# Seven products of blocks for eight in the second layer's first MLP product, with its sums on VectorE and its squares on ScalarE

## The chip, the cores and the metric

The kernel runs on one core of one Trainium2 chip. The metric is device time in microseconds, the median of the runs of the kernel; lower is better. The engines are called by the names of the profile: PE (TensorE, matmuls), DVE (VectorE), ACT (ScalarE), POOL (GpSimd) and SP (SyncE, which here issues DMAs).

## The reference

One inference step of a backbone of two layers, in float32. There are 640 tokens: 512 latent ones and 128 of context, each group with its own modulation. The model width is 1024, the hidden width of the MLP 4096.

```python
def squared_relu_mlp(h, w1, w2):
    return jnp.square(jax.nn.relu(h @ w1)) @ w2

def modulate(x, g, shift, scale):
    return rmsnorm(x, g) * (1 + scale) + shift

def trunk_layer(x, mod, p, mix_fn):
    shift1, scale1, gate1, shift2, scale2, gate2 = jnp.split(mod, N_MOD, axis=-1)
    y, ctx_state = mix_fn(modulate(x, p['norm1'], shift1, scale1))
    x = x + gate1 * y
    x = x + gate2 * squared_relu_mlp(modulate(x, p['norm2'], shift2, scale2), p['w1'], p['w2'])
    return x, ctx_state
```

`mix_fn` holds four groups of heads (a convolution, a spatial gate, latent attention and windowed attention) between one input and one output projection. After the second layer comes a last norm. The change concerns `h @ w1` of the second layer, the squares behind it, and the norm and modulation that make its `h`.

## The kernel before

Features lie on partitions and tokens on columns: `x` and the modulated `h` are eight tiles of 128 features by 640 tokens. The tokens are worked on in two parts, `HALVES = ((0, 384), (384, 256))`.

Every operand of a matmul is kept as two tensors, a high part (the value rounded to the matmul's format) and a low part (what the rounding left). `mm3` (L239 to L243) issues three matmuls for a product: high by high (L241), high by low (L242), low by high (L243). One product of 128 by 128 weights thus costs three matmuls. `load_unit` (L228 to L234) brings 128 x 1024 weights by a DMA from SP into a `raw` tile (three buffers), casts them on ACT (L232) and subtracts on DVE (L233), or on POOL where `pool` is set, into an `hl` tile (four buffers) that holds both parts.

The MLP of a layer works in eight portions of 512 hidden features. `mlp1(j)` (L1072) makes four hidden tiles of 128 in both token parts: 24 matmuls a tile and part into a PSUM bank `w1`, then `mlp1_tile` (L1059) takes relu on ACT (L1067), squares once on POOL (L1068, full precision) and once on ACT (L1069, the high part), and subtracts on DVE (L1070, the low part). `mlp2(j)` (L1099) multiplies the four tiles with the second weights into the eight feature tiles of the output, again by parts, and `gate_add` (L383 to L386) adds each result times the gate to `x` on DVE. The loop at L1119 issues `mlp1(j + 1)` ahead of `mlp2(j)`, so that PE has a portion of the first product to do while the other engines make the low parts of the one before. `Modulate.step` (L334) makes `h` for one feature tile and one token part: two or one products on DVE (L350), the high part on ACT, the low part on DVE (L358). The second token part's steps stand behind the first tile of `mlp1(0)`.

Results in PSUM come from the pools `mm`, `fl` and `s2` with two buffers each; one of `s2` holds two banks. The program is written in the order of the stages, and a scheduler of the tile framework sets the order in each engine's queue by the dependences and by a model of durations. On the chip each engine then runs its own queue in that order and waits by semaphores.

## Time and profile before

| what | value |
| --- | --- |
| median of three runs | 1562.17 us |
| the three runs | 1557.77, 1564.02, 1562.17 us |
| span of the profiled execution | 1557.7 us |
| PE busy | 1491.2 us, 96% of the span |
| PE weight loads (beside PE) | 1434.7 us |
| DVE busy | 1034.4 us, 66% |
| ACT busy | 612.0 us, 39% |
| POOL busy | 293.3 us, 19% |

The span and the busy times come from one profiled execution, whose own time lies with the lowest of the three runs. Matmuls overlap in the pipeline, so the duration of one PE row is longer than the time that it adds; starts tell the pace. A row's bracket names how long the engine was idle just before it and which work released it. The second layer's MLP lies at about 1088 to 1548 us of the span.

### The profile page before, as it was taken

What the parts mean: (1) busy time and instruction counts of PE and PEld (TensorE: products, weight loads), DVE (VectorE), ACT (ScalarE), POOL (GpSimd) and SP (SyncE); (2) the same over time, 40 slices, a digit from 0 to 9 for tenths busy, and PEclk for the clock granted to TensorE, in tenths of its full rate; (3) what the DMA queues carried; (4) which work ended last, traced back from release to release, by engine and by line L of the source; (5) the groups of instructions that cost most, each with busy time, mean ns of one, the idle gap of its engine ahead of it and who ended that gap; (6) DMA issues with size and microseconds to landing.
All of it is one profiled execution on the core that took longest, in us unless ns stands there. A gap on an engine that the chain in (4) does not pass through costs nothing. (4 is left out here: it accounts for less than half of the span.)

```text
span 1557.7 us, 25473 instructions
## 1 busy us (share of the span) xinstructions
PE 1491.2 (96%) x9884; PEld 1434.7 (92%) x9884; DVE 1034.4 (66%) x2051; ACT 612.0 (39%) x1324; POOL 293.3 (19%) x309
## 2 busy tenths in 40 slices
PE   6898999989999999999999999998999999999997
PEld 2698989979999999999999988997999999999997
DVE  5988878869988777876467676776643433443444
ACT  3544556744222231222246455774532223223221
POOL 2133103343210110110021120224211011001002
PEclk9899999999999999999999999999999999999998
DMA  8544321323555444444212311021222222222211
GB/s 309 197 136 138 99 71 45 90 87 111 184 161 162 145 151 151 149 148 137 75 48 70 116 42 35 28 72 63 87 69 82 68 82 69 81 76 74 78 45 68
DMA packets 49816, 159.52 MB, mean 102 GB/s; under 512 B 6176, under 2 KB 10272, under 8 KB 49696
## 3 DMA queue, kind: packets, MB, share of 16 engines
q1 hardware_dynamic: 48032, 153.96, 30.7%
q10 hardware_dynamic: 1664, 3.93, 0.7%
q8 instruction: 78, 1.28, 0.3%
q14 instruction: 42, 0.34, 0.1%
HBM read 154.82 MB, written 3.05 MB: 101 GB/s over the span
## 5 line engine op out<-in xcount | busy, mean ns | idle before, releaser
L232 ACT CAST hl<-raw 128x1024 fp32r<-128x1024 f32 (+3 forms) x204 | 200.1, 983 | 400.4 <-PE w L243 320.1
L242 PE MATMUL w<-h,hl 128*128 128x256 f32 (+1 forms) x1024 | 317.3, 311 | 6.6 <-DVE h L358 6.6
L241 PE MATMUL w<-u,hl 128*128 128x384 f32 (+1 forms) x1024 | 317.4, 310 | 3.6 <-DVE x L386 3.5
L243 PE MATMUL w<-h,hl 128*128 128x256 f32 (+1 forms) x1024 | 317.9, 310 | 0.0
L243 PE MATMUL w<-u,hl 128*128 128x384 f32 (+1 forms) x1024 | 317.0, 310 | 0.0
L242 PE MATMUL w<-u,hl 128*128 128x384 f32 (+1 forms) x1024 | 316.9, 309 | 0.0
L241 PE MATMUL w<-h,hl 128*128 128x256 f32 (+1 forms) x1024 | 316.7, 310 | 0.0
L233 DVE TENSOR_TENSOR hl<-raw,hl 128x1024 fp32r<-128x1024 f32 (+3 forms) x184 | 216.0, 1176 | 106.4 <-ACT hl L232 106.1
L1068 POOL TENSOR_TENSOR rq<-rr 128x384 f32<-128x384 f32 (+1 forms) x128 | 110.0, 860 | 676.3 <-ACT rr L1067 629.3
L386 DVE SCALAR_TENSOR_TENSOR x<-w,mod,x 128x128 f32<-128x128 f32 (+1 forms) x384 | 154.8, 434 | 109.7 <-PE w L243 109.0
L242 PEld LDWEIGHTS w<-h,hl 128*128 128x128 f32 x1024 | 195.0, 190 | 8.3 <-DVE h L358 8.2
L241 PEld LDWEIGHTS w<-u,hl 128*128 128x128 f32 x1024 | 194.2, 190 | 4.5 <-DVE x L386 4.1
L243 PEld LDWEIGHTS w<-h,hl 128*128 128x128 f32 x1024 | 195.0, 190 | 0.0
L241 PEld LDWEIGHTS w<-h,hl 128*128 128x128 f32 x1024 | 194.9, 190 | 0.0
L242 PEld LDWEIGHTS w<-u,hl 128*128 128x128 f32 x1024 | 194.4, 190 | 0.0
L243 PEld LDWEIGHTS w<-u,hl 128*128 128x128 f32 x1024 | 194.2, 190 | 0.0
L167 DVE CUSTOM_DVE_ANT_0 junk<-adaw,cb,vec 128x1024 f32<-128x1024 f32 x84 | 115.3, 1373 | 65.5 <-DMA adaw<-in_wada 65.5
L1067 ACT ACTIVATE rr<-w 128x384 f32<-128x384 f32 (+1 forms) x128 | 55.9, 436 | 250.2 <-PE w L243 250.2
L1070 DVE TENSOR_TENSOR u<-rq,u 128x384 fp32r<-128x384 f32 (+1 forms) x128 | 67.8, 530 | 92.7 <-POOL rq L1068 92.6
L167 DVE CUSTOM_DVE_ANT_0 adaw<-adaw,cb,vec 128x1024 f32<-128x1024 f32 x84 | 115.1, 1370 | 1.3
L241 PE MATMUL fm<-h,hl 128*128 128x256 f32 (+1 forms) x288 | 92.2, 320 | 2.1 <-DVE u L533 2.1
L242 PE MATMUL fm<-h,hl 128*128 128x256 f32 (+1 forms) x288 | 90.0, 313 | 0.0
(264 smaller groups left out, 2571.2 us busy)
## 6 DMA issues: line engine op xcount, KB each, us to landing
raw<-in_wf SPq DMA_DIRECT2D x146, 512.0 KB, 3.5
adaw<-in_wada SPq DMA_DIRECT2D x84, 512.0 KB, 3.8
raw<-in_wo SPq DMA_DIRECT2D x24, 384.0 KB, 3.1
adan<-in_wnat SPq DMA_DIRECT2D x12, 512.0 KB, 8.4
raw<-in_wt SPq DMA_DIRECT2D x16, 384.0 KB, 3.2
x<-in_xT ACTq DMA_DIRECT2D x4, 640.0 KB, 7.5
raw<-in_wt SPq DMA_DIRECT2D x8, 288.0 KB, 2.9
raw<-in_wo SPq DMA_DIRECT2D x4, 512.0 KB, 3.7
```

What stands on the lines that cost most here:

```text
L167: nc.vector.tensor_tensor_reduce(out=raw if g else junk, in0=raw, in1=cb[:, g, :], op0=ALU.mult, op1=ALU.add, scale=1.0, scalar=vecs[l][:, ...
L232: nc.scalar.copy(hl[:, 0, :n], raw[:, :n])
L233: (nc.gpsimd if pool else nc.vector).tensor_sub(hl[:, 1, :n], raw[:, :n], f(hl[:, 0, :n]))
L241: nc.tensor.matmul(out, lhsT=lhs[0], rhs=rhs[0], start=start, stop=False)
L242: nc.tensor.matmul(out, lhsT=lhs[0], rhs=rhs[1], start=False, stop=False)
L243: nc.tensor.matmul(out, lhsT=lhs[1], rhs=rhs[0], start=False, stop=stop)
L386: nc.vector.scalar_tensor_tensor(out=x[:, m, t0:t0 + n], in0=ps[:, t0 - b0:t0 - b0 + n], scalar=mods[l][g][:, gate + m:gate + m + 1], in1= ...
L1067: nc.scalar.activation(r, ps[:, :n], AF.Relu)
L1068: nc.gpsimd.tensor_mul(q, r, r)
L1070: nc.vector.tensor_sub(ui[:, 1, t0:t0 + n], q, f(hh))
```

## The change

In the second layer, hidden tiles are taken in pairs, `Pair(p)` with p from 0 to 15. Pairs 0 and 1 stay plain. Pairs 2 to 15 use the scheme of Strassen in Winograd's form: the 1024 features are split in two halves of four tiles, the 640 tokens in two halves of 320 (`HT`), and the pair's two tiles are the two halves of the third dimension. Of a pair's eight products of blocks seven are left; each is 4 x 3 = 12 matmuls of 320 columns. The names of their moving operands are `b11`, `b21`, `b22` (halves of `h` itself), `t1`, `t2`, `t3` and `t4` (sums of halves).

- `Blocks` (a subclass of `Modulate`): `keep()` reserves space for `h` in full precision, one tile of it in the constant `cb`, and `step` then issues one more pass on ACT for each high part of `h`. `sums(s)`, for s from 0 to 3, makes the four sums on DVE and splits each into high part (ACT) and low part (DVE); the sum `t4` overwrites a quarter of `h`.
- `Pair.load` brings a pair's two units of weights; `w1` and `w2` make four weight tiles from them, with four sums of 128 x 512 on DVE: `wa` (raw), `ws23`, `ws14` (sums) and `w22` (128 x 512). They use the four `hl` buffers.
- `first`, `second` and `rest` issue the seven products into PSUM banks `qa`, `qb` and the double bank `qcd`, two of them on top of another. DVE adds and subtracts the products to the four blocks of the result, ACT takes relu; `square` makes both squares on ACT over 640 columns and the low part on DVE.
- `full(p)` issues a whole pair. The loop: two plain pairs, the sums, `mlp2(0)`, pairs 2 and 3, and then pair 2j + 2, `mlp2(j)`, pair 2j + 3.
- Plain pairs of the second layer square on ACT twice instead of on POOL and ACT. The first layer keeps POOL.
- In both layers the second modulation and the plain tiles go through the feature tiles in the order `K_PAIRS`. The constants `msk` and `rq` are loaded once in each layer, and pools are opened and closed by phase so that the MLP has space of its own (`me`).

The diff, cut to its core:

```diff
+K_PAIRS = (0, 4, 1, 5, 2, 6, 3, 7)
...
+                if self.hf is not None:
+                    nc.scalar.activation(self.hf[k % 4][:, k // 4, t0:t0 + n], t[:, o:o + n], AF.Identity,
+                                         bias=shift)
...
+    class Blocks(Modulate):
...
+        def sums(self, s):
+            if s == 0:
+                self.op = {k: [None] * 4 for k in ("b11", "b21", "b22", "t1", "t2", "t3", "t4")}
+            op = self.op
+            if s % 2 == 0:
+                t3 = phase["me"].tile([128, 2, 2, HT], F32R, tag="t3", bufs=1, name=nm("t3")) if s else \
+                    tb([128, 2, 2, HT], "t3")
+                for k, two in (("t2", ta([128, 2, 2, HT], "t2")), ("t3", t3), ("t1", ta([128, 2, 2, HT], "t1"))):
+                    op[k][s], op[k][s + 1] = two[:, 0], two[:, 1]
+            h1, h2 = self.h[s], self.h[4 + s]
+            op["b11"][s], op["b21"][s], op["b22"][s] = h1[:, :, :HT], h2[:, :, :HT], h2[:, :, HT:]
+            op["t4"][s] = h1[:, :, HT:]
+            fx = self.hf[s]
+            b11, b12, b21, b22 = fx[:, 0, :HT], fx[:, 0, HT:], fx[:, 1, :HT], fx[:, 1, HT:]
+            t3, t2_ = tmp2([128, HT], "t3"), tmp2([128, HT], "t2")
+            nc.vector.tensor_sub(t3, b12, b22)
+            nc.vector.tensor_sub(b12, b11, b12)
+            nc.vector.tensor_add(t2_, b22, b12)
+            nc.vector.tensor_sub(b21, b21, t2_)
+            for k, src in (("t2", t2_), ("t3", t3), ("t1", b12), ("t4", b21)):
...
-            nc.gpsimd.tensor_mul(q, r, r)
...
+            def plain(self, us, i, half, tail=None):
...
+                hh = ui[:, 0, t0:t0 + n]
+                nc.scalar.activation(r, ps[:, :n], AF.Relu)
+                nc.scalar.activation(hh, r, AF.Square)
+                if blocks:
+                    nc.scalar.activation(q, r, AF.Square)
+                else:
+                    nc.gpsimd.tensor_mul(q, r, r)
+                nc.vector.tensor_sub(ui[:, 1, t0:t0 + n], q, f(hh))
+            def load(self):
+                self.raw = []
+                for i in range(2):
+                    raw = rawp.tile([128, 2, 512], F32, tag="raw", name=nm("raw"))
+                    nc.sync.dma_start(out=raw, in_=wf[l, U_W1 + 2 * self.p + i].rearrange("p (a b) -> p a b", a=2))
+                    self.raw.append(raw)
+            def hl(self, src, n=2):
+                t = hlp.tile([128, 2, 2, 512], F32R, tag="hl", name=nm("hl"))
+                split(t[:, 0, :n], t[:, 1, :n], src)
+                return t
+            def w1(self):
+                self.wa = self.hl(self.raw[0])
+            def w2(self):
+                r1, r2 = self.raw
+                s23 = me.tile([128, 2, 512], F32, tag="s", bufs=2, name=nm("s"))
+                s14 = me.tile([128, 2, 512], F32, tag="s", bufs=2, name=nm("s"))
+                nc.vector.tensor_add(s14[:, 0], r2[:, 0], r2[:, 1])
+                nc.vector.tensor_add(s23[:, 0], r1[:, 0], s14[:, 0])
+                nc.vector.tensor_add(s23[:, 1], r1[:, 0], r2[:, 0])
+                nc.vector.tensor_add(s14[:, 1], r1[:, 1], s23[:, 0])
+                self.ws23 = self.hl(s23)
+                self.ws14 = self.hl(s14)
+                self.w22 = self.hl(r2[:, 1:2], 1)
+            def mul(self, ps, w, i, op, start):
+                for s in range(4):
+                    c = slice(128 * s, 128 * s + 128)
+                    b = mod.op[op][s]
+                    mm3(ps, (w[:, 0, i, c], w[:, 1, i, c]), (b[:, 0, :], b[:, 1, :]), start and s == 0, s == 3,
+                        not start)
+            def first(self):
+                self.a = bank("qa")[:, :HT]
+                self.mul(self.a, self.wa, 0, "b11", True)
+                self.q1 = me.tile([128, HT], F32, tag="q1", bufs=1, name=nm("q1"))
+                nc.scalar.copy(self.q1, self.a)
+            def second(self):
+                self.mul(self.a, self.wa, 1, "b21", False)
+                self.r[0] = tp([128, TOK], "rr")
+                nc.scalar.activation(self.r[0][:, :HT], self.a, AF.Relu)
+            def square(self, i):
+                r, u = self.r[i], self.u[i]
+                nc.scalar.activation(u[:, 0, :], r, AF.Square)
+                nc.scalar.activation(r, r, AF.Square)
+                nc.vector.tensor_sub(u[:, 1, :], r, f(u[:, 0, :]))
+            def rest(self):
+                bv = bank("qb")[:, :HT]
+                cd = bank2("qcd")
+                c, d = cd[:, 0, :HT], cd[:, 1, :HT]
+                self.mul(bv, self.ws23, 0, "t2", True)
+                v, w = tmp2([128, HT], "V"), tmp2([128, HT], "W")
+                nc.vector.tensor_sub(v, bv, self.q1)
+                self.mul(c, self.ws23, 1, "t3", True)
+                nc.vector.tensor_add(w, c, v)
+                self.second()
+                self.mul(d, self.ws14, 0, "t1", True)
+                r0, r1 = self.r[0], tp([128, TOK], "rr")
+                self.r[1] = r1
+                nc.vector.tensor_sub(r1[:, HT:], w, d)
+                self.mul(c, self.w22, 0, "t4", False)
+                nc.vector.tensor_add(r1[:, :HT], c, v)
+                nc.scalar.activation(r1, r1, AF.Relu)
+                self.square(1)
+                self.mul(d, self.ws14, 1, "b22", False)
+                nc.vector.tensor_sub(r0[:, HT:], d, v)
+                nc.scalar.activation(r0[:, HT:], r0[:, HT:], AF.Relu)
+                self.square(0)
+        def full(p):
+            x_ = Pair(p)
+            x_.load()
+            x_.w1()
+            x_.w2()
+            x_.first()
+            x_.rest()
+            return x_.u
...
-        prev = mlp1(0)
-        for j in range(8):
-            cur = prev
-            if j < 7:
-                prev = mlp1(j + 1)
-            mlp2(j, cur)
+        head = [Pair(p, None if blocks else [ta([128, 2, TOK], "u") for _ in range(2)]) for p in range(2)]
+        ws = [load_unit(wf[l, U_W1 + i], pool=True) for i in range(4)]
+        for half in range(2):
+            for i in range(4):
+                head[i // 2].plain(ws[2 * (i // 2):2 * (i // 2) + 2], i % 2, half)
+                if half == 0 and i == 0:
+                    for k in K_PAIRS:
+                        mod.step(1, k)
+        us = head[0].u + head[1].u
+        if blocks:
+            for s in range(4):
+                mod.sums(s)
+            mlp2(0, us)
+            us = full(2) + full(3)
+            for j in range(1, 8):
+                if j < 7:
+                    nxt_us = full(2 * j + 2)
+                mlp2(j, us)
+                if j < 7:
+                    us = nxt_us + full(2 * j + 3)
+            close_phase()
+            del phase["me"]
+        else:
+            for j in range(8):
+                cur = us
+                if j < 7:
+                    us = two_plain(j + 1)
+                mlp2(j, cur)
```

In the order of PE the first place is the joint between two pairs, pair 7 to pair 8. Before, at the joint between `mlp1(j + 1)` and `mlp2(j)`, the rows are these (`w1`, `w2`: PSUM tiles of the two products; `h`, `u`: their moving operands; `hl`: weights):

```order
L242 MATMUL w1_2040_14124<-h_1719_11446,hl_2036_14090 128x256
L243 MATMUL w1_2040_14124<-h_1719_11446,hl_2036_14090 128x256
L241 MATMUL w2_2045_14160<-u_1947_13359,hl_2044_14157 128x384 [waits Activation_49]
L242 MATMUL w2_2045_14160<-u_1947_13359,hl_2044_14157 128x384
L243 MATMUL w2_2045_14160<-u_1947_13359,hl_2044_14157 128x384 [waits DVE_49]
```

Now `qcd_1964` is the double bank of pair 7 and `qa_1979` the first bank of pair 8, whose weights are `hl_1973`; `hl_1960` is pair 7's tile `w22`:

```order
L249 MATMUL qcd_1964_13346<-t1_1784_11866,hl_1959_13324 128x320
L250 MATMUL qcd_1964_13346<-t1_1784_11866,hl_1959_13324 128x320
L248 MATMUL qa_1979_13461<-h_1703_11348,hl_1973_13443 128x320 [waits Activation_49]
L249 MATMUL qa_1979_13461<-h_1703_11348,hl_1973_13443 128x320
L250 MATMUL qa_1979_13461<-h_1703_11348,hl_1973_13443 128x320 [waits DVE_49]
...
L248 MATMUL qa_1979_13461<-h_1725_11464,hl_1973_13443 128x320
L248 MATMUL qcd_1964_13346<-h_1703_11348,hl_1960_13327 128x320 [waits DVE_49]
L249 MATMUL qcd_1964_13346<-h_1703_11348,hl_1960_13327 128x320
```

Before, the next product's weights are another buffer of four that come one at a time; now the ten matmuls that need the next pair's first weights stand between the sixth and the seventh product, t1 and t4, of the pair before, behind a wait for the cast (ACT) and one for the low part (DVE).

In the order of ACT the second place is the joint between pair 8 and the second product of portion 3. Before, at such a joint the casts of weights (L232) stand like this among the passes of `mlp1` (L1067, L1069):

```order
L232 CAST hl_2012_13889<-raw_2011_13887 128x1024 [waits DMAHW6_49,PE_49]
L232 CAST hl_2020_13956<-raw_2019_13954 128x1024 [waits DMAHW7_49,PE_49]
L232 CAST hl_2028_14023<-raw_2027_14021 128x1024 [waits DMAHW0_49,DVE_49,PE_49]
L232 CAST hl_2036_14090<-raw_2035_14088 128x1024 [waits DMAHW1_49,DVE_49,PE_49]
L1067 ACTIVATE rr_2014_13917<-w1_2013_13892 128x384 [waits PE_49,Pool_49]
L1069 ACTIVATE u_2007_13883<-rr_2014_13917 128x384 [waits Activation_49]
```

Now, from the cast of pair 8's `ws14` (`hl_1977`) to that of the second product's first weights (`hl_1988`); `rr_1967` and `rr_1968` are what relu is taken of in pair 7, `u_1951` and `u_1952` its results:

```order
L253 CAST hl_1977_13455<-s_1975_13447 128x1024 [waits DVE_49,PE_49]
L1215 ACTIVATE rr_1968_13401<-rr_1968_13401 128x640 [waits DVE_49]
L1186 COPY q1_1980_13474<-qa_1979_13461 128x320 [waits PE_49,Activation_49]
L1195 ACTIVATE u_1952_13307<-rr_1968_13401 128x640 [waits Activation_49]
L253 CAST hl_1978_13458<-raw_1972_13441 128x512 [waits DMAHW1_49,PE_49]
L1196 ACTIVATE rr_1968_13401<-rr_1968_13401 128x640 [waits Activation_49]
L1219 ACTIVATE rr_1967_13387<-rr_1967_13387 128x320 [waits DVE_49]
L1195 ACTIVATE u_1951_13306<-rr_1967_13387 128x640 [waits Activation_49]
L1196 ACTIVATE rr_1967_13387<-rr_1967_13387 128x640 [waits Activation_49]
L239 CAST hl_1988_13570<-raw_1987_13568 128x1024 [waits DMAHW2_49,PE_49]
```

Where four casts followed one another, the cast of the second product's first weights now stands behind the seven passes and the short cast that follow `hl_1977`, which itself waits for PE.

In the order of DVE the third place is the start of the MLP of the second layer, ahead of the low part of the second product's first weights. Before (`u`: results of `mlp1(0)`; `h_1719`: the last tile of `h`):

```order
L1070 TENSOR_TENSOR u_1722_11452<-rq_1748_11596,u_1722_11452 128x384 [waits Pool_49]
L358 SCALAR_TENSOR_TENSOR h_1719_11446<-mt_1745_11563,mod1_123,h_1719_11446 128x128 [waits Activation_49] x2
L1070 TENSOR_TENSOR u_1723_11453<-rq_1751_11627,u_1723_11453 128x384 [waits Pool_49]
L1070 TENSOR_TENSOR u_1724_11454<-rq_1754_11658,u_1724_11454 128x384 [waits Activation_49,Pool_49]
L233 TENSOR_TENSOR hl_1772_11793<-raw_1771_11791,hl_1772_11793 128x1024 [waits DMAHW6_49,PE_49,Activation_49]
L1070 TENSOR_TENSOR u_1721_11451<-rq_1757_11689,u_1721_11451 128x256 [waits Activation_49,Pool_49]
```

Now (`hl_1790` are the second product's first weights; L254 is the low part in `split`, L415 to L418 are the sums of `Blocks.sums`, L1145 the low part of a plain tile):

```order
L254 TENSOR_TENSOR t3_1782_11864<-t3_1785_11867,t3_1782_11864 128x320 [waits Activation_49]
L415 TENSOR_TENSOR t3_1787_11881<-hf_1702_11347 128x320 [waits DVE_49]
L1145 TENSOR_TENSOR u_1731_11483<-rq_1771_11797,u_1731_11483 128x256 [waits Activation_49]
L254 TENSOR_TENSOR h_1703_11348<-cb_89,h_1703_11348 128x320 [waits Activation_49]
L254 TENSOR_TENSOR h_1713_11405<-hf_1700_11345,h_1713_11405 128x320 [waits Activation_49]
L254 TENSOR_TENSOR t1_1784_11866<-hf_1701_11346,t1_1784_11866 128x320 [waits Activation_49]
L254 TENSOR_TENSOR h_1721_11452<-hf_1701_11346,h_1721_11452 128x320 [waits Activation_49]
L416 TENSOR_TENSOR hf_1702_11347<-hf_1702_11347 128x320 [waits DVE_49]
L254 TENSOR_TENSOR t3_1782_11864<-t3_1787_11881,t3_1782_11864 128x320 [waits Activation_49]
L417 TENSOR_TENSOR t2_1788_11882<-hf_1702_11347 128x320 [waits DVE_49]
L240 TENSOR_TENSOR hl_1790_11897<-raw_1789_11895,hl_1790_11897 128x1024 [waits DMAHW0_49,Activation_49]
```

Ahead of the first low part of weights for PE's next stage there are now the sums of `h` and their low parts, of which the last are shown.

## Rows read from the trace of the kernel before

**Rows 1.** Page, span and part 1: busy us, share of the span, instructions.

```profile
span 1557.7 us, 25473 instructions
...
PE 1491.2 (96%) x9884; PEld 1434.7 (92%) x9884; DVE 1034.4 (66%) x2051; ACT 612.0 (39%) x1324; POOL 293.3 (19%) x309
```

**Rows 2.** A stretch of the second MLP: busy us (instructions) by engine, clock, DMA.

```profile
1250.00:1300.00 50.00, 50.00 (x343) 50.00 (x342) 20.72 (x37) 12.88 (x21) 4.82 (x7) 1.00 0.23 74
```

**Rows 3.** PE in order of time, one tile pair: start us, duration us.

```profile
1298.73 0.34 PE L241 MATMUL w<-h,hl 128*128 128x384 f32 x1
...
1302.89 0.28 PE L241 MATMUL w<-h,hl 128*128 128x256 f32 x1
...
1305.76 0.34 PE L241 MATMUL w<-h,hl 128*128 128x384 f32 x1
```

**Rows 4.** PE in order of time, three matmuls of 320 columns and the next.

```profile
990.60 0.31 PE L241 MATMUL S<-kk,qq 128*128 128x320 f32 x1
...
991.04 0.28 PE L242 MATMUL out<-y,hl 128*128 128x256 f32 x1
```

**Rows 5.** DVE groups by shape, whole run: busy us, mean ns, idle before.

```profile
L233 DVE TENSOR_TENSOR hl<-raw,hl 128x1024 fp32r<-128x1024 f32 x144 | 179.5, 1248 | 96.7 <-ACT hl L232 96.6
...
L386 DVE SCALAR_TENSOR_TENSOR x<-w,mod,x 128x384 f32<-128x384 f32 x128 | 78.5, 613 | 64.6 <-PE w L243 64.6
L386 DVE SCALAR_TENSOR_TENSOR x<-w,mod,x 128x128 f32<-128x128 f32 x256 | 77.6, 345 | 45.1 <-PE w L243 44.4
...
L626 DVE TENSOR_TENSOR ct<-ct,fm 128x384 f32<-128x384 f32 x4 | 2.2, 554 | 1.7 <-PE fm L243 1.7
L247 DVE TENSOR_TENSOR y<-cy,y 128x640 fp32r<-128x640 f32 x4 | 3.3, 818 | 0.0
...
L233 DVE TENSOR_TENSOR hl<-raw,hl 128x512 fp32r<-128x512 f32 x4 | 2.8, 688 | 4.9 <-ACT hl L232 4.9
```

**Rows 6.** ACT groups by shape, whole run, same columns.

```profile
L232 ACT CAST hl<-raw 128x1024 fp32r<-128x1024 f32 x152 | 159.1, 1048 | 367.3 <-PE w L243 317.2 <-DMA raw<-in_wf 29.5 <-PE fm L243 8.7
L1069 ACT ACTIVATE u<-rr 128x384 fp32r<-128x384 f32 x64 | 33.6, 525 | 1.9
...
L1069 ACT ACTIVATE u<-rr 128x256 fp32r<-128x256 f32 x64 | 26.8, 419 | 0.1
...
L628 ACT ACTIVATE cy<-ct,vec 128x640 f32<-128x640 f32 x4 | 3.3, 823 | 0.0
...
L246 ACT CAST y<-cy 128x640 fp32r<-128x640 f32 x4 | 2.9, 723 | 3.1 <-DVE cy L639 3.1
...
L232 ACT CAST hl<-raw 128x512 fp32r<-128x512 f32 x4 | 2.6, 639 | 0.8 <-PE tm L243 0.7
```

**Rows 7.** PE in order of time: the matmul that ends a weight buffer's use.

```profile
1214.26 0.28 PE L243 MATMUL w<-u,hl 128*128 128x256 f32 x1
```

**Rows 8.** ACT in order of time: the cast that waited for that matmul.

```profile
1214.58 1.05 ACT L232 CAST hl<-raw 128x1024 fp32r<-128x1024 f32 x1 [5.39 <-PE w L243]
```

**Rows 9.** DVE in order of time: low part behind a cast.

```profile
1300.34 1.23 DVE L233 TENSOR_TENSOR hl<-raw,hl 128x1024 fp32r<-128x1024 f32 x1 [2.18 <-ACT hl L232]
```

**Rows 10.** ACT in order of time, the cast ahead of it.

```profile
1299.27 1.04 ACT L232 CAST hl<-raw 128x1024 fp32r<-128x1024 f32 x1
1300.21 0.42 ACT L1069 ACTIVATE u<-rr 128x256 fp32r<-128x256 f32 x1
```

**Rows 11.** PE in order of time, start of the second MLP.

```profile
1091.36 0.45 PE L242 MATMUL w<-h,hl 128*128 128x384 f32 x1 [2.39 <-DVE h L358]
```

**Rows 12.** Stretches with idle PE, columns as in rows 2.

```profile
345.00:350.00 5.00, 2.61 (x16) 2.11 (x14) 5.00 (x7) 2.16 (x5) 3.10 (x2) 1.00 0.48 128
350.00:355.00 5.00, 3.60 (x21) 3.04 (x20) 4.91 (x7) 2.65 (x4) 2.37 (x1) 1.00 0.33 116
...
1090.00:1095.00 5.00, 3.23 (x13) 2.91 (x14) 4.91 (x8) 2.47 (x4) 2.54 (x2) 0.75 0.53 184
1095.00:1100.00 5.00, 5.00 (x19) 5.00 (x18) 3.93 (x7) 1.23 (x2) 1.43 (x2) 0.57 0.32 105
```

109 lines of the change are left out of this document (63 added, 46 removed).

## The prediction

> **What bounds the kernel now.** I read the page's part 1 first, for the share of each engine. PE is busy 1491.2 of the 1557.7 us of the span [rows 1]. Then I cut the second layer's MLP into stretches: in 50 us there, PE is busy for all 50 at the full clock, DVE for 20.7, ACT for 12.9 [rows 2]. So in this stage time is PE's number of matmuls times their pace, and whatever other engines do is hidden as long as it arrives before PE asks for it. Two things decide: how many microseconds of matmul go, and whether the new work on ACT and DVE makes PE wait where it never waited.
>
> Durations of PE rows overlap, so the pace is taken from starts. Twenty-four matmuls of 384 columns take 1302.89 - 1298.73 = 4.16 us, or 0.1733 each; the next twenty-four of 256 columns take 1305.76 - 1302.89 = 2.87 us, or 0.1196 each [rows 3]. The three of 320 columns in an attention stage take 991.04 - 990.60 = 0.44 us, or 0.147 each [rows 4], which lies in the middle of the other two.
>
> **What goes.** A pair is two hidden tiles of 128. Plain, it takes 48 matmuls of 384 and 48 of 256: 48 x 0.1733 + 48 x 0.1196 = 14.06 us. By products it takes 7 x 4 x 3 = 84 matmuls of 320: 84 x 0.147 = 12.35 us. That is 1.71 us a pair, and 14 of the 16 pairs of the second layer change: 23.9 us less.
>
> The Trainium skill ("TensorE: Matmul & The Clock Gate", section Back-to-back issue gap) gives the gap of a lone matmul at the full clock as its columns over 2.4 plus 2.5 ns. By it a product pair would take 84 x 135.8 ns = 11.41 us, a plain one 13.04 us, and the change would be worth 22.9 us instead of 23.9. The trace has 11 to 12 ns above columns over 2.4 at all three sizes [rows 3, 4], so the rows' price is used.
>
> **What comes, by volume.** For two pairs and one eighth of the second part, 52.7 us of PE, DVE now has: eight weight sums of 512 at 0.688, six low parts of 1024 at 1.248 and two of 512 at 0.688, ten of 320 out of PSUM (at most 0.554, the row of 384), four low parts of 640 at 0.818, and for the second part four low parts of 1024 and eight times 0.613 + 2 x 0.345 [rows 5]. Together 38.6 us, 73% of the time, from 41%. ACT has ten casts of 1024 at 1.05, two of 512 at 0.64 [rows 6], ten passes over 640 and six over 320. No row shows a square over 640 from SBUF: the cast takes 0.723, a pass with a vector scale 0.823, and the squares of 384 and 256 (0.525 and 0.419) lead to 0.735, which I take; 320 then takes 0.47. That makes 22 us. GpSimd's squares go, and nothing waited for it that PE waited for. By volume all is hidden; the order is what costs.
>
> **What comes, by order.** Four weight buffers (hl) hold all four weights of a product pair, so the next pair's can be cast only when PE has left the buffer. From PE's last matmul to the cast's start I count 0.2 us after the matmul's pace ends: it starts at 1214.26, the cast at 1214.58 [rows 7, 8]. The low part starts 0.03 after the cast's end [rows 9, 10]: 1.05 + 0.03 + 1.23. For a signal back to PE and the weight load I take 0.1, an estimate; no row shows PE waiting for weights in this stage.
>
> First joint, pair to pair. The first weights of the second pair take the buffer that the first pair leaves after its fourth product. PE then has one product and two matmuls that need only the high part, 14 x 0.147 = 2.06 us, against 0.2 + 1.05 + 0.03 + 1.23 + 0.1 = 2.61. PE waits 0.6 us. This is so at six places (pairs 2, 5, 7, 9, 11 and 13): 3.6 us.
>
> Second joint, product pair to second part (and pair 3 to 4, the third in a row). ACT's row, as the order shows, holds the cast of the pair's third weights, which waits for the previous pair's last product; behind it stand relu, q1, square, a cast of 512, square, relu, two squares, and then the cast of the second part's first weights. With 0.09 saved where one does not depend on the one before (1300.21 is 0.94 after 1299.27 [rows 10]) this is 0.2 + 0.94 + 0.63 + 0.33 + 0.63 + 0.54 + 0.63 + 0.47 + 0.63 + 0.63 + 1.05 = 6.7 us. PE has 45 matmuls beside it, 6.6 us, then two with the high part (0.35); then it waits for the low part, 0.03 + 1.23 + 0.1. I get 0.2 + 1.0 = 1.2 us at seven places, 8.4 us. If 640 costs 0.823, five passes add 0.45 to each: 3.2 us more. If the cast came first in the row the joint would cost 0.6, as the last one does (pair 15, no pair in front): 0.6.
>
> The end. The last eighth of the second part needs the last pair at once. After pair 15's last product come subtraction, relu, a cast in front, two squares and a low part of 640: 0.7 + 0.47 + 0.94 + 0.73 + 0.65 + 0.85 = 4.3 us, of which 15 matmuls of 0.173 hide 2.6; with the split of the wait 1.9 us are left. Before, the last quarter of u was made while PE did other work.
>
> The start. The two plain pairs cover 32 activations more on ACT (24 us of PE hide them in volume), but the order puts 15 sums and 13 low parts of 320 (at 0.4 to 0.5, between the rows of 256 and 384) and six low parts of u on DVE, 12.6 to 16 us, ahead of the low part of the second part's first weights. PE's last four plain tiles are 4 x 2.87 = 11.5 us. Four of the casts overwrite h and must wait for the last plain tile anyway. I get a wait of 2 to 8 us and take 4. The wait ahead of the first plain tile (2.39 us [rows 11]) stays by size, later by ACT's extra passes and earlier by the order of k: 0, with 3 either way. In the first layer only the order of k changes, and in both layers the place of two loads of constants, which lie under tens of us of other work: 0, with 2 either way.
>
> **Sum.** -23.9 + 3.6 + 8.4 + 0.6 + 1.9 + 4.0 = -5.4 us. The span of 1557.7 is that of a fast run: the three runs have 1557.8, 1562.2 and 1564.0, so the profiled execution stands 4.5 us below the median. The forecast is 1552.3 for such an execution and 1556.5 on the scale of the median, in 1551 to 1562.
>
> **Rivals.**
>
> *The joints do not show.* If PE's order leaves more beside the casts than I count, only start and end remain: -23.9 + 4.0 + 1.9 = -18, or 1544. For it: DVE is idle half the time now [rows 2]. Against it: the casts wait for buffers, not for an engine.
>
> *The clock falls at the joints.* This one ends on the other side. After PE sat idle 2.39 us [rows 11] the granted clock was 0.75 and 0.57 in the next two stretches, the lower of the two levels (1.2 GHz) for part of them, and a stretch of 5 us held 19 matmuls where 29 would fit [rows 12]: about 3.4 us a time. At four of the seven longer joints that is 13.6: +8, or 1570. It decides from the second such joint on. Against it: the same place in layer 0 idled 5.00 - 2.61 and 5.00 - 3.60 us in two stretches with the clock at 1.00 [rows 12], and my joints idle at most 1.2 at once. The Trainium skill ("TensorE: Matmul & The Clock Gate", section A second HAM failure mode: psum-queue depth-cycling) tells of short idles between groups of matmuls that make the clock swing. By that rule this rival would be the forecast; the rows of layer 0 speak against it.
>
> *DVE falls behind at the start and stays so.* With 73% to do it needs most of an eighth to recover. If the start costs 12 instead of 4: +2.6, or 1565.
>
> **Chances.** Forecast 0.50, joints hidden 0.22, clock 0.13, DVE behind 0.15. A difference under 0.5% (7.8 us) can't be told from none here. Faster by more takes the hidden joints and the lower third of the forecast's range: 0.40. Slower takes the clock and a little of the third rival: 0.16. Between: 0.44. The range that leaves out no more than 2 in 10 is 1543 to 1570.
>
> **What would show it.** Right: matmuls of 320 columns at 0.147 from start to start; PE idle of 0.6 and about 1.2 us twice in each period of some 54.5 us, put down to the low part of a weight (DVE) and to its cast (ACT); a gap of 2 to 8 us ahead of the first tile of the second part; PE full otherwise. Wrong: a period near 52.7 us (joints hidden) or above 56 us, a clock below 1.00 in the middle of the stage, gaps that DVE's subtractions out of PSUM end, or matmuls of 320 at another pace.

## The result: 1.2% faster, below the stated range

The changed kernel takes 1542.26 us (median of four runs, 1537.63 to 1548.54), the kernel before 1560.06 in the same comparison; the ratio is 0.988, with a 95% interval of 0.9861 to 0.9899. That is 18 us, where the sum had said 5.4 (and the figure of 1556.5 beside it 5.7), and 0.7 us below the lower end of the range. It is the outcome of the first rival, the joints that do not show, at 1544. Run again later, the changed kernel gave 0.9883 (0.9863 to 0.9904).

The page of the changed kernel, span and part 1, against [rows 1]:

```profile
span 1542.1 us, 25203 instructions
...
PE 1473.7 (96%) x9716; PEld 1415.8 (92%) x9716; DVE 1131.9 (73%) x2210; ACT 668.9 (43%) x1400; POOL 248.2 (16%) x245
```

168 matmuls fewer (14 pairs times 12), and PE is as full as before. The stretches of the second MLP that answer to [rows 2, 12], two at its second part's start, and one whole period of two pairs and an eighth of the second part (columns: length, then PE, PEld, DVE, ACT and POOL busy, granted clock, DMA share, GB/s):

```profile
1250.00:1300.00 50.00, 50.00 (x339) 49.59 (x338) 32.27 (x56) 17.49 (x25) 0.00 (x0) 1.00 0.25 83
1090.00:1095.00 5.00, 3.63 (x18) 2.68 (x16) 4.66 (x8) 3.88 (x7) 2.02 (x2) 1.00 0.32 105
1095.00:1100.00 5.00, 3.53 (x19) 2.90 (x20) 4.97 (x8) 3.26 (x7) 4.10 (x3) 1.00 0.42 128
1120.00:1125.00 5.00, 3.43 (x28) 3.22 (x28) 5.00 (x14) 5.00 (x15) 0.00 (x0) 1.00 0.00 0
1125.00:1130.00 5.00, 4.58 (x19) 4.37 (x19) 4.69 (x9) 3.45 (x7) 0.00 (x0) 0.70 0.32 105
1203.00:1256.00 53.00, 53.00 (x361) 52.59 (x360) 34.90 (x59) 20.62 (x28) 0.00 (x0) 1.00 0.25 80
```

In the middle PE shows no idle, though 50 us hold a whole joint between two pairs and one to the second part; DVE went from 20.7 to 32.3 us, ACT from 12.9 to 17.5. The idle that there is lies at the start: in 1090 to 1100 while the norm and the first tiles of `h` are made, and at 1120 to 1130, in the first half of which ACT and DVE are busy without a break.

To place the difference I took PE's starts through the whole stage, from the first matmul of the second MLP to the last, and subtracted the pace (0.1733, 0.1467 and 0.1193 us for 384, 320 and 256 columns). What is left over is summed in four parts: the first 20 us (head); from there to 12 us behind the second part's first matmul (start); the last 40 us (end); the rest (middle). All in us, one profiled execution each; the third row is a second execution of the changed kernel, and the rows below it are the experiments.

| kernel | stage | at pace | head | start | middle | end |
| --- | --- | --- | --- | --- | --- | --- |
| before | 458.7 | 450.1 | 7.0 | 0.1 | 0.4 | 1.1 |
| changed | 441.3 | 426.2 | 4.8 | 4.1 | 2.9 | 3.2 |
| changed, again | 441.3 | 426.4 | 4.7 | 4.1 | 2.9 | 3.2 |
| buffers in rotation | 440.5 | 426.3 | 6.1 | 0.1 | 4.7 | 3.3 |
| casts three times | 460.2 | 426.4 | 4.7 | 4.1 | 21.8 | 3.2 |
| squares on GpSimd | 442.5 | 426.2 | 5.7 | 4.5 | 2.9 | 3.2 |
| sums later | 439.6 | 426.1 | 7.2 | 0.3 | 2.9 | 3.2 |
| end, other order | 441.8 | 426.4 | 5.5 | 3.9 | 2.9 | 3.2 |
| before, order of k | 458.8 | 450.2 | 7.1 | 0.1 | 0.4 | 1.0 |
| weight sums on GpSimd | 442.2 | 426.4 | 7.1 | 2.5 | 3.1 | 3.2 |
| sums later, GpSimd at the end | 436.6 | 426.3 | 4.7 | 0.3 | 2.9 | 2.4 |
| the same, again | 438.9 | 426.3 | 7.0 | 0.3 | 2.9 | 2.4 |
| the same, modulation later | 437.9 | 426.3 | 6.0 | 0.3 | 3.0 | 2.4 |

So the stage is 17.4 us shorter, and the parts give it: -23.9 of matmuls, +4.0 start, +2.5 middle, +2.1 end, -2.2 head. The rest of the program is 1.8 us longer in this execution (the stage begins at 1089.8 instead of 1087.6; in the second execution of the changed kernel it begins at 1087.8).

### The profile page after: what moved, and what is told of

It reads as the page before. It is cut to its first block, busy times and chain, and to the rows that moved or that the text cites. A ratio compares the mean times of both kernels' runs of the same rounds, so it can differ in the third digit from the quotient of the medians.

```text
span 1542.1 us, 25203 instructions
## 1 busy us (share of the span) xinstructions
PE 1473.7 (96%) x9716; PEld 1415.8 (92%) x9716; DVE 1131.9 (73%) x2210; ACT 668.9 (43%) x1400; POOL 248.2 (16%) x245
## 4 chain that ended last, share of the span: by engine, by line
PE 78%; DVE 11%; ACT 4%; issue 2%; POOL 1%; DMA 1%; POOLq 0%; DVEq 0%; ACTq 0%; SPq 0%
PE w L250 13%; PE w L249 13%; PE w L248 13%; PE qcd L248 2%; PE fm L248 2%; PE qcd L250 2%; PE fm L250 2%; PE qcd L249 2%; PE fm L249 2%; PE out L248 2%; PE tm L249 2%; PE tm L248 2%; PE tm L250 2%; PE out L249 2%; PE out L250 2%
## 5 line engine op out<-in xcount | busy, mean ns | idle before, releaser
L239 ACT CAST hl<-raw 128x1024 fp32r<-128x1024 f32 (+3 forms) x176 | 170.7, 973 | 267.3 <-PE w L250 155.8
L240 DVE TENSOR_TENSOR hl<-raw,hl 128x1024 fp32r<-128x1024 f32 (+3 forms) x156 | 182.7, 1174 | 36.8 <-ACT hl L239 36.4
L249 PE MATMUL w<-h,hl 128*128 128x384 f32 (+1 forms) x576 | 178.4, 311 | 3.8 <-DVE h L369 3.8
L250 PE MATMUL w<-h,hl 128*128 128x384 f32 (+1 forms) x576 | 178.3, 310 | 0.0
L248 PE MATMUL w<-h,hl 128*128 128x384 f32 (+1 forms) x576 | 177.7, 310 | 0.0
L270 POOL TENSOR_TENSOR ss<-ss,sq 128x384 f32<-128x384 f32 (+1 forms) x40 | 37.3, 932 | 502.3 <-ACT sq L269 501.6
L1144 POOL TENSOR_TENSOR rq<-rr 128x384 f32<-128x384 f32 (+1 forms) x64 | 65.1, 1018 | 328.9 <-ACT rr L1139 273.3
L249 PEld LDWEIGHTS w<-h,hl 128*128 128x128 f32 x576 | 109.4, 190 | 5.7 <-DVE h L369 5.7
L248 PEld LDWEIGHTS w<-h,hl 128*128 128x128 f32 x576 | 109.6, 190 | 0.0
L250 PEld LDWEIGHTS w<-h,hl 128*128 128x128 f32 x576 | 109.6, 190 | 0.0
L248 PE MATMUL fm<-h,hl 128*128 128x256 f32 (+1 forms) x288 | 93.8, 326 | 2.1 <-DVE u L582 2.1
L249 PE MATMUL fm<-h,hl 128*128 128x256 f32 (+1 forms) x288 | 91.6, 318 | 0.0
L250 PE MATMUL fm<-h,hl 128*128 128x256 f32 (+1 forms) x288 | 91.4, 317 | 0.0
```

What stands on the lines that cost most here:

```text
L239: nc.scalar.copy(hl[:, 0, :n], raw[:, :n])
L240: (nc.gpsimd if pool else nc.vector).tensor_sub(hl[:, 1, :n], raw[:, :n], f(hl[:, 0, :n]))
L248: nc.tensor.matmul(out, lhsT=lhs[0], rhs=rhs[0], start=start, stop=False, skip_group_check=more)
L249: nc.tensor.matmul(out, lhsT=lhs[0], rhs=rhs[1], start=False, stop=False, skip_group_check=more)
L250: nc.tensor.matmul(out, lhsT=lhs[1], rhs=rhs[0], start=False, stop=stop, skip_group_check=more)
L270: (nc.gpsimd if pool else nc.vector).tensor_add(self.s[:, t0:t0 + n], self.s[:, t0:t0 + n], sq[:, :n])
```

## Where the joints went

The joint between pairs 7 and 8. In PE's order the products of a pair write `qa`, `qb`, `qcd`, `qa`, `qcd`, `qcd`, `qcd`; so those of t1 and t4, which the section on the change calls the sixth and the seventh, are the fifth and the sixth here. ACT of the changed kernel in order of time, the casts of pair 8's first weights (from `raw`) and second weights (from `s`):

```profile
1279.68 1.05 ACT L253 CAST hl<-raw 128x1024 fp32r<-128x1024 f32 x1 [3.09 <-PE qcd L250]
1281.44 0.44 ACT L1191 ACTIVATE rr<-qa 128x320 f32<-128x320 f32 x1 [0.71 <-PE qa L250]
1281.78 1.04 ACT L253 CAST hl<-s 128x1024 fp32r<-128x1024 f32 x1
...
1286.59 1.05 ACT L253 CAST hl<-s 128x1024 fp32r<-128x1024 f32 x1 [3.78 <-PE qcd L250]
...
1292.28 1.05 ACT L239 CAST hl<-raw 128x1024 fp32r<-128x1024 f32 x1
```

DVE, the low part of pair 8's first weights and that of the second part's first:

```profile
1280.76 1.23 DVE L254 TENSOR_TENSOR hl<-raw,hl 128x1024 fp32r<-128x1024 f32 x1 [0.59 <-ACT hl L253]
...
1293.42 1.22 DVE L240 TENSOR_TENSOR hl<-raw,hl 128x1024 fp32r<-128x1024 f32 x1
```

And PE: the start of the fourth product (`qa`), the matmul that needs the first low part, the end of the sixth product (the matmul before 1286.39), and the one that needs the second:

```profile
1279.48 0.31 PE L248 MATMUL qa<-h,hl 128*128 128x320 f32 x1
...
1283.30 0.31 PE L250 MATMUL qa<-h,hl 128*128 128x320 f32 x1
...
1286.39 0.31 PE L249 MATMUL qa<-h,hl 128*128 128x320 f32 x1
...
1295.95 0.34 PE L250 MATMUL w<-u,hl 128*128 128x384 f32 x1
```

The cast at 1279.68 starts 0.2 us after the *third* product ends (1279.48), not the fourth, which ends at 1281.24. The next pair's first weights took the buffer of the third product, which ends the use of `ws23`, and the cast of its second weights, at 1281.78, the one of the fourth, which ends the use of `wa`. The low part is there at 1281.99; PE asks for it at 1283.30, so 1.3 us are to spare. At the other joint the cast of the third weights (1286.59) waits for the sixth product, not the seventh. From it to the end of the cast at 1292.28 + 1.05 are 6.74 us, as forecast (6.7), but PE has 62 matmuls of 320 and two of 384 in front of 1295.95 instead of the 45 and two I counted; again 1.3 us to spare. At the other joints of both kinds 1.1 to 1.4 us are to spare.

## Experiments

**Buffers in fixed rotation.** Does the spare time come from the buffer's order? The edit in short; the second MLP opens a pool of its own for the four buffers:

```diff
-        hl = hlp.tile([128, 2, 1024], F32R, tag="hl", ...)
+        n += 1; hl = hlp.tile([128, 2, 1024], F32R, tag=f"hl{n % 4}", ...)   # bufs=1 each, second MLP
```

> The four weight buffers of the second layer's MLP are used in fixed rotation, as the prediction had assumed, instead of going to the next user in the order in which they come free. Theory A (the forecast's joints were wrong because a buffer comes free one product, 12 x 0.147 = 1.76 us, earlier than assumed): the cast of the next pair's first weights starts right behind the pair's fourth product instead of its third, the cast of the third weights behind the seventh product instead of the sixth. The scheduler has put 19 instead of 14 matmuls between the fourth product's end and the first one that needs the low part (2.8 us against 2.6), so nothing is lost there; at the joint to the second part 45 matmuls of 0.147 and 7 of 0.173 stand against 6.7 + 1.26 + 0.1, so PE waits 0.2 to 0.4 us at seven places: 1 to 3 us slower than the changed kernel, some 1544. Rival B (the joints are hidden whatever the buffers do, by engines being quicker than counted): the casts start as early as in the changed kernel, no wait on PE, 1542.

Measured 1549.58 us, 0.9909 of before (0.9883 to 0.9935), an interval that overlaps that of the changed kernel. In its profile 5.4 us more lie ahead of the stage (it begins at 1095.2, in the changed kernel at 1089.8), among them a wait of 1.49 us of PE for the first weights; the stage of the other versions, with the changed kernel's program ahead of it, begins between 1086.3 and 1094.8. ACT, DVE and then PE at the same joint:

```profile
1283.34 1.05 ACT L268 CAST hl<-s 128x1024 fp32r<-128x1024 f32 x1 [3.14 <-PE qcd L265]
...
1285.39 1.04 ACT L268 CAST hl<-raw 128x1024 fp32r<-128x1024 f32 x1
...
1286.46 1.23 DVE L269 TENSOR_TENSOR hl<-raw,hl 128x1024 fp32r<-128x1024 f32 x1 [0.81 <-ACT hl L268]
```

```profile
1287.49 0.31 PE L264 MATMUL qb<-t,hl 128*128 128x320 f32 x1
1287.74 0.41 PE L265 MATMUL qa<-h,hl 128*128 128x320 f32 x1
1287.99 0.31 PE L263 MATMUL qa<-h,hl 128*128 128x320 f32 x1
```

The first weights' cast (from `raw`) now comes behind the fourth product, which ends at 1284.86, 2.3 us after the third product's end (1283.10) instead of 0.2. Its low part is ready at 1286.46 + 1.23 = 1287.69. PE would have asked for it at 1287.64, one pace behind 1287.49, and starts at 1287.74, 0.10 us late; the next matmul is late by 0.10 again. The spare 1.3 us are used up, although the scheduler, which sees the later buffer, put five more matmuls in front. At the joint to the second part the weights that PE asks for first are now cast behind the fourth product of pair 8 (the cast starts at 1298.02, behind the relu of `qa`). DVE, then PE there:

```profile
1299.09 1.23 DVE L255 TENSOR_TENSOR hl<-raw,hl 128x1024 fp32r<-128x1024 f32 x1 [0.81 <-ACT hl L254]
...
1300.18 0.28 PE L263 MATMUL w<-u,hl 128*128 128x256 f32 x1
1300.37 0.45 PE L265 MATMUL w<-u,hl 128*128 128x384 f32 x1
1300.65 0.34 PE L263 MATMUL w<-u,hl 128*128 128x384 f32 x1
```

Here the low part ends at 1300.32 and PE starts 0.07 us late, with 0.11 more behind it. Each of the two is so at six places, and the joint from pair 3 to 4 waits 0.30 us for a cast; the middle is 1.8 us longer than in the changed kernel. That is A, in its range of 1 to 3 us, with waits smaller than counted at the second joint and some at the first, where none was expected. B falls: the casts start later and PE waits for what hangs on them. Fixed rotation would still not have made my forecast of 12.6 us at the joints true, because the scheduler reorders around the later buffer. The stage as a whole is no longer than the changed kernel's (440.5 against 441.3), because the start fell from 4.1 to 0.1; there the cast of the second part's first weights (1127.47) stands ahead of the casts of `h` in ACT's row (from 1129.03), where in the changed kernel (1123.71) it stands behind three of them.

**Casts three times.** Does a joint cost anything when the chain is longer than its cover?

```diff
+                for _ in range(2):      # in Pair.hl, and so in load_unit for the second part
+                    nc.scalar.copy(t[:, 0, :n], src)
                 split(t[:, 0, :n], t[:, 1, :n], src)
```

> In the second layer's MLP every cast of weights of the product pairs, and of the second part from its second eighth on, is done three times on ACT (the same values). Theory A (PE waits at a joint by what the cast and the low part take beyond the matmuls ahead of the first that needs them; the changed kernel has 1.3 us to spare there): at the joint between two pairs the chain from the third product's end is 0.2 + 0.94 + 0.94 + 0.33 + 1.05 + 0.03 + 1.23 + 0.1 = 4.8 us against 26 matmuls of 0.147 or 3.8: PE waits 1.0 us at six places for the low part. At the joint to the second part the cast of its first weights now stands behind a relu that waits for PE, with five casts: some 1.6 us at seven places. Together 17 us more than the changed kernel, some 1559, with 8 to 30. Rival B (joints are hidden by volume: ACT is busy for 12 of 25 us and can take more): no waits on PE at the joints, 1542.

Measured 1561.02 us, 0.9997 of before (0.9976 to 1.0017). What PE waited for in the middle (us in total, times, longest):

```profile
PE qa L251 <- DVE hl L255: 4.2, 6, 0.7
PE qcd L249 <- DVE rr L1215: 4.0, 6, 0.7
PE qcd L249 <- DVE rr L1217: 3.5, 6, 0.6
PE qa L249 <- ACT q L1189: 1.9, 1, 1.9
```

B falls: ACT is busy for 36 to 39 of 50 us and PE waits. The first line is the joint between pairs, 0.7 where 1.0 was expected, at the six places named. The forecast total came out (the middle is 18.9 us longer, 17 expected), but in part by luck: no wait for the second part's weights appears, which A had put at 1.6 us at seven places. Instead the two last products of six pairs wait for DVE's passes over the product before them, since the second part's matmuls that had stood between them (nine and five in the changed kernel) were moved behind. A joint does cost what a chain has beyond its cover, and the scheduler decides where it is paid.

The same run judges the rival of the clock. A stretch with such waits (the four after it read 1.00 too; the one from 1150 to 1200, with the idle of 1.9 us, read 0.97):

```profile
1250.00:1300.00 50.00, 48.97 (x331) 48.49 (x332) 32.42 (x55) 35.69 (x45) 0.00 (x0) 1.00 0.23 75
```

Idle times of 0.6 to 0.7 us, three in each period of 56 us, left the clock at its upper level. The prediction weighed what the Trainium skill ("TensorE: Matmul & The Clock Gate", section A second HAM failure mode: psum-queue depth-cycling) tells of, short idles between groups of matmuls that make the clock swing; no run here shows that at such idle times.

**Sums behind the first eighth of the second part.**

```diff
+            mlp2(0, us)
             for s in range(4):
                 mod.sums(s)
-            mlp2(0, us)
```

> The four sums of h are issued behind the first eighth of the second part instead of ahead of it. Theory A (the queue of sums ahead of the first weights' cast and low part makes the start's waits): both waits (1.57 and 0.42 us) and the lower clock behind them go, 3 to 3.6 us less than the changed kernel. Rival B (the sums are only late elsewhere): PE waits ahead of pair 2 for the last sums, as much or more.

Measured 1540.60 us, 0.9861 (0.9844 to 0.9877). The start fell from 4.1 to 0.3 us, and no wait came ahead of pair 2: A. In its profile the head was 2.4 us longer, with the waits of 0.73 and 1.82 and the clock at 0.50 in 1095 to 1100 (more on this below). Its runs are not told from those of the changed kernel, whose interval overlaps.

**Squares of the plain pairs on GpSimd.**

```diff
-                nc.scalar.activation(q, r, AF.Square)
+                nc.gpsimd.tensor_mul(q, r, r)
```

> The plain pairs 0 and 1 of the second layer square on GpSimd again (8 passes fewer on ACT around the start of the second layer's MLP). Theory A (the start's wait of 1.57 us for the cast on ACT comes from ACT's queue): eight squares of 0.42 to 0.53 us leave ACT, 3.8 us, so the cast comes in time, and the wait of 1.57, that of 0.42 and the 1.5 us of lower clock behind them go: 3 us less than the changed kernel. Rival B (DVE, busy without a break there, is slowed by GpSimd's passes): the low part of the first weights comes later, the wait moves from the cast to the low part and grows, 0 to 4 us more.

Measured 1544.91 us, 0.9888 (0.9868 to 0.9909), the start 4.5 us instead of 4.1. PE there, then what the second row waited for:

```profile
1128.12 0.39 PE L248 MATMUL w<-u,hl 128*128 128x256 f32 x1 [0.15 <-ACT u L1140]
1130.40 0.39 PE L249 MATMUL w<-u,hl 128*128 128x256 f32 x1 [1.90 <-DVE u L1142]
...
1127.53 2.36 POOL L1141 TENSOR_TENSOR rq<-rr 128x256 f32<-128x256 f32 x1 [2.76 <-issue]
1129.92 0.42 DVE L1142 TENSOR_TENSOR u<-rq,u 128x256 fp32r<-128x256 f32 x1 [0.51 <-POOL rq L1141]
```

The wait for the cast went, as A said, and one of 1.90 us for the low part of `u` took its place, so the 3 us were not won. It is not B's either: DVE was idle 0.51 us in front of that low part, and what came late was GpSimd's own square of the last plain tile, 2.36 us where the three before it took 0.66 to 0.89. What helped at the start was less work ahead of PE's next need, as in the experiment above.

**The end, matmuls of pair 14 first.**

```diff
+                for m in range(4):      # k = 0, 1 of four output tiles into four banks
+                    ...
+                for m in range(4):      # then k = 2, 3
```

> In the last eighth of the second part the matmuls that need only pair 14 are issued for four output tiles (24 matmuls, 4.2 us) before the first that needs pair 15. Theory A (the end's waits of 0.75 and 0.67 us are the chain behind pair 15's last product): they go, 1.4 to 1.9 us less than the changed kernel. Rival B (the norm at the very end is set by another chain): the waits go and the end comes no sooner.

Measured 1543.89 us, 0.9882 (0.9859 to 0.9906); the waits stayed at 0.75 and 0.66. The edit changed nothing there: PE's rows of the last stretch stand in the same order in both kernels, with these 24 matmuls ahead of the first wait already in the changed one, so neither A nor B was put to the test. It serves as another run of the changed kernel's second MLP.

**The kernel before with the new order of k.**

```diff
-            for k in range(KT):
+            for k in (0, 4, 1, 5, 2, 6, 3, 7):
```

> The kernel before, with only the order of the feature tiles (0, 4, 1, 5, 2, 6, 3, 7) in the second modulation and the tiles of the first part in both layers. Theory A (the start of the second MLP is 2 us shorter in the changed kernel because of this order): PE's time over its pace in the first 20 us of that MLP falls from 7.0 to about 4.8 us. Rival B (it is the clock, which in one execution falls after the idle there and in another doesn't): idle of some 2.8 us stays with either order, with or without 2.5 us of lower clock behind it. Either way the time is within 3 us of the kernel before.

Measured 1562.47 us, 1.0005 (0.9988 to 1.0021). Head 7.1 against 7.0, waits of 2.40 and 0.42 as before: the order of k is not what shortened the head. A falls, and B's idle of 2.8 us is there.

**Sums of weights on GpSimd.**

```diff
-                nc.vector.tensor_add(s14[:, 0], r2[:, 0], r2[:, 1])
+                nc.gpsimd.tensor_add(s14[:, 0], r2[:, 0], r2[:, 1])     # and the other three
```

> The four sums of weights of each product pair (128 x 512) run on GpSimd instead of DVE. Theory A (DVE's volume is no bound, 55 to 80% busy in this stage, and GpSimd is idle): no change, within 1 us. Rival B (GpSimd's passes hold up DVE's passes with two operands in SBUF, as at 1088.5 us of the kernel before, where a subtraction of 0.5 us beside one of GpSimd took 2.47): low parts come up to 2 us later, more than the 1.3 us to spare at the joints, so PE waits up to 0.7 us at thirteen joints: up to 9 us more.

Measured 1547.12 us, 0.9902 (0.9883 to 0.9922). DVE's groups of 1150 to 1500 us (busy us, mean ns):

```profile
L1197 DVE TENSOR_TENSOR u<-rr,u 128x640 fp32r<-128x640 f32 x26 | 27.1, 1043 | 1.0 <-ACT rr L1196 1.0
L254 DVE TENSOR_TENSOR hl<-raw,hl 128x1024 fp32r<-128x1024 f32 x13 | 19.1, 1473 | 3.5 <-ACT hl L253 3.5
```

In the changed kernel:

```profile
L1197 DVE TENSOR_TENSOR u<-rr,u 128x640 fp32r<-128x640 f32 x26 | 21.4, 821 | 1.0 <-ACT rr L1196 1.0
L254 DVE TENSOR_TENSOR hl<-raw,hl 128x1024 fp32r<-128x1024 f32 x13 | 15.9, 1221 | 3.5 <-ACT hl L253 3.5
```

These two groups are slower beside GpSimd's passes, as B said, but by 0.2 to 0.3 us in the mean, under the 1.3 to spare, and the middle stays at 3.1 us: no wait at a joint, which is A's outcome there. What the run shows beyond that lies outside the stage or at its head.

**GpSimd for the last weights, sums later, and again with the changed kernel.** The line below comes on top of the edit that moves the sums; with `all_pool`, `load_unit` casts and subtracts on GpSimd.

```diff
-                us = [load_unit(wf[l, U_W2 + 4 * j + i]) for i in range(4)]
+                us = [load_unit(wf[l, U_W2 + 4 * j + i], all_pool=blocks and i > 1) for i in range(4)]
```

> Sums of h behind the first eighth of the second part, and in the last eighth the weights of the last four output tiles are cast and subtracted on GpSimd, which has nothing to do there, instead of on ACT and DVE. Theory A (the end's waits come from a cast of 0.93 us and a low part of 1.2 us that stand in the rows of ACT and DVE ahead of the last pair's square and low part): the waits of 0.75 and 0.67 us at the end go, beside those at the start: 5 us less than the changed kernel, stage 1.4 us under that with only the sums moved. Rival B (GpSimd's passes slow DVE's or come too late for the last four tiles): a new wait there of 1 us or more takes their place.

> The changed kernel itself, again, beside the two below on the same chip. Theory A (its 18 us are -23.9 of matmuls, +4 at the start, +2 at the end, +2.5 at the joints, and a start of the MLP that by the granted clock is 0 or 2.3 us shorter than before): 0.988 of the kernel before, the second layer's MLP 441 to 444 us from the first to the last of its matmuls. Rival B (part of the gain is the execution that was profiled): 0.991 or more.

> Sums behind the first eighth and the last weights on GpSimd, again: by the profiles its MLP is 4.5 us shorter where the clock does not fall, so 0.985 of the kernel before. Rival: what is won at the start and the end is less than executions differ by, 0.987 to 0.988.

Measured 1541.24 us, 0.9871 (0.9848 to 0.9894); again, beside the changed kernel on one chip, 1539.41, 0.9861 (0.9837 to 0.9884), against 1542.36, 0.9883. At the end the wait of 0.75 us went and that of 0.67 stayed: half of A. The changed kernel's second measurement is its A (0.9883, the stage 441.3 us); that of this version, 0.9861, lies between its forecast of 0.985 and the rival's 0.987. By the table this version is 4.6 us shorter than the changed kernel in start and end, in both profiles; by the runs 3 us, which their intervals do not separate. It beats the kernel before clearly, the changed kernel not measurably.

**Modulation of the second token part one tile later.** On top of the version above.

```diff
-                if half == 0 and i == 0:
+                if half == 0 and i == (1 if blocks else 0):
```

> The same, with the second token part's modulation behind the second plain tile instead of the first. Theory A (PE stops 1.8 us for the norm's sum because its matmul stands early in PE's row): 13 matmuls more stand ahead of it, the wait goes, 1.8 us less than the one above, and no idle that a lower clock could follow. Rival B (the modulation of the second token part comes too late for the plain tiles of that part): a wait of 1 to 5 us there.

Measured 1541.52 us, 0.9869 (0.9842 to 0.9895). PE at the head:

```profile
1092.71 0.61 PE L290 MATMUL rb<-ones,ss 128*128 128x1 f32 x4 [0.20 <-DVE ss L270]
1093.18 0.42 PE L248 MATMUL w<-h,hl 128*128 128x384 f32 x1
...
1095.35 0.44 PE L249 MATMUL w<-h,hl 128*128 128x384 f32 x1 [1.57 <-DVE h L369]
```

The wait for the norm fell from 1.83 to 0.20 us, and a wait of 1.57 for the low part of `h` of the first token part came right behind it: in these rows PE waits for DVE, whichever product asks first. Neither A nor B.

## Why the prediction was wrong, step by step

*What goes, -23.9: right.* At pace the stage went from 450.1 to 426.2. The 320 columns run at 0.1467. The text put the trace at 11 to 12 ns above columns over 2.4; its own rows give 13.

*First and second joint, +3.6, +8.4 and +0.6: this step failed.* "The first weights of the second pair take the buffer that the first pair leaves after its fourth product", and the third weights' cast "waits for the previous pair's last product": both took the four buffers to go round in fixed order. In the changed kernel they go to the next user as they come free, so each cast starts one product, 12 x 0.147 = 1.76 us, earlier. -0.6 of spare time becomes +1.2 (1.3 measured); for the second joint -1.2 becomes +0.6 (1.3 measured, by five more matmuls). The durations of the chains were right: 2.61 against 2.5 measured, 6.7 against 6.74. PE waited for weights at no joint, and the period is 53.2 us (the cast at 1279.68 has its like at 1226.50), near the 52.7 that the prediction gave as the sign of hidden joints; with the fixed order forced, the spare time was gone and PE did wait. The order of PE, ACT and DVE was read row by row; which product frees a buffer was assumed. For the 0.1 us of a signal back to PE the rows now show 0.05 to 0.06 from the end of the pass on DVE to the start of the matmul that waits, and 0.10 more ahead of the next one.

*By volume all is hidden: right*, at 66% DVE and 39% ACT over a whole period (1203 to 1256), where 73% and 42% had been counted.

*The start, +4: right in place, and in size in part by luck.* Of the 4.0 us 1.57 are the wait for the cast, 0.42 that for the low part and 0.3 the restarts behind them; some 1.6 are the lower clock (0.70), which the step did not have. In the profile of the weight sums on GpSimd, with the same two waits, the clock read 1.00 from 1125 to 1135 and the start cost 2.5. PE of the changed kernel:

```profile
1124.80 0.45 PE L248 MATMUL w<-u,hl 128*128 128x384 f32 x1 [1.57 <-ACT hl L239]
...
1126.67 0.45 PE L250 MATMUL w<-u,hl 128*128 128x384 f32 x1 [0.42 <-DVE hl L240]
```

The forecast had DVE's queue of sums alone as the cause. The longer wait was for ACT's cast, and moving the sums cured both.

*The end, +1.9: right.* 2.1 us; the waits, PE of the changed kernel:

```profile
1504.53 0.96 PE L248 MATMUL w<-u,hl 128*128 128x384 f32 x4 [0.75 <-ACT u L1195]
1506.16 0.44 PE L249 MATMUL w<-u,hl 128*128 128x384 f32 x1 [0.67 <-DVE u L1197]
```

*The head, 0 with 3 either way: -2.2, and it belongs to the execution.* The waits of 2.39 us [rows 11] and 0.41 became three of 0.74, 1.83 and 0.20: 2.8 us in both. But in [rows 12] the clock fell behind it, and in the two profiles of the changed kernel it did not; with the sums moved later and the same waits, it did.

*In the middle 2.5 us* that no step had: in the 13 pairs that lie in it, the first matmul of the sixth and of the seventh product starts up to 0.06 us late, and the next follows 0.04 to 0.11 us behind its pace. DVE, then PE of the changed kernel at the sixth product of pair 7:

```profile
1283.99 0.48 DVE L1212 TENSOR_TENSOR rr<-W,qcd 128x320 f32<-128x320 f32 x1
...
1284.32 0.31 PE L248 MATMUL qa<-h,hl 128*128 128x320 f32 x1
1284.53 0.42 PE L248 MATMUL qcd<-h,hl 128*128 128x320 f32 x1
1284.78 0.32 PE L249 MATMUL qcd<-h,hl 128*128 128x320 f32 x1
```

PE would have started at 1284.47 and starts at 1284.53, 0.06 us behind the end of DVE's subtraction out of the same double bank (1284.47). At 14 of the 26 places the start follows such a subtraction at the same distance: waits for DVE's pass over the product before, too short for a bracket, and the same ones that grew to 0.6 and 0.7 us with the casts done three times. At the other 12 the pass ends 0.07 to 0.12 us ahead and only the second matmul is late; that the cause is the same there is not shown. The prediction had gaps that DVE's subtractions out of PSUM end among the signs of being wrong, but at no price.

*The scale, +4.5 for the median: a span was compared with times.* In every run that lists both, the span is 1.7 to 2.2 us shorter than the time of the same run: the changed kernel's profiled execution has a span of 1542.1 and a time of 1544.02, 1.8 above its median of 1542.26. The span of 1557.7 thus belongs to a time of some 1559.7 (an estimate from these differences), near the median of 1560.06 and not at the lowest run. So 15.6 us by the spans became 17.8 by the medians mostly because the changed kernel's profile is one of its longer executions. The sum of -5.4 also leads to 1556.8 from the median of 1562.17, and not to 1556.5.

With the joints at 0 the sum would have been -23.9 + 1.9 + 4.0 = -18, which is what the first rival says. That the stage came out so near (-17.4) is in part luck, since the middle's +2.5 and the head's -2.2 were in neither sum. The rival had 0.22; what was written for it, that more stands beside the casts than counted, is what the trace shows, and what was written against it, that the casts wait for buffers, is true and not enough.

## What to carry to other kernels

When a cast waits for a buffer, do not assume which one: find the release in the trace or the waits of the cast, since one product more or less of cover (here 1.76 us) decided in this forecast between 12.6 us and nothing. A scheduler that sees a later buffer reorders around it: forcing the assumed order by hand brought back 1.8 us in the middle, lengthening the chain 18.9. Ahead of a change of stage, move work that is not needed yet behind the next stage's first loads; moving the squares to another engine only moved the wait.

## What the hardware did that was not expected

The same program, with the same waits up to the same matmul, kept the clock in one execution and lost it in the next. PE and clock in the head of the version with both edits, its first profile and its second:

```profile
1100.00:1105.00 5.00, 3.56 (x19) 2.92 (x20) 4.97 (x8) 3.26 (x7) 4.07 (x3) 1.00 0.43 121
1105.00:1110.00 5.00, 5.00 (x32) 5.00 (x31) 4.43 (x15) 3.95 (x12) 0.00 (x0) 1.00 0.22 88
```

```profile
1100.00:1105.00 5.00, 3.75 (x13) 3.75 (x14) 4.97 (x7) 3.29 (x7) 4.13 (x3) 0.63 0.44 124
1105.00:1110.00 5.00, 5.00 (x23) 5.00 (x23) 3.14 (x11) 1.70 (x5) 0.00 (x0) 0.68 0.21 86
```

Both executions idled 0.74 and 1.83 us just before; the fall cost 2.3 us (head 4.7 and 7.0), where the prediction's rival had taken 3.4. The four runs of the changed kernel follow their mean granted clock: 0.987, 0.985, 0.981 and 0.978 go with 1537.6, 1540.5, 1544.0 and 1548.5 us. The start shows the same: with waits of 1.57 and 0.42 us the clock fell in the changed kernel (start 4.1), and with waits of 1.57 and 0.41 it stayed at 1.00 in the version with the weight sums on GpSimd (start 2.5). So a single profile can hold some 2 us at such an idle that the change has nothing to do with, and a difference of that size needs the waits, not the time, to be believed.
